# Moving three row loads and 28 operand loads in the queues of a streaming encoder's down projection

## The chip, the core and the metric

The kernel runs on one core of a Trainium2 chip. The metric is device time in microseconds (us) of one execution; three runs of the kernel before gave 2360.87, 2361.01 and 2362.78, a median of 2361.01. A core has a matmul engine (PE, with its weight loads as PEld), VectorE (DVE), ScalarE (ACT), GpSimd (POOL) and SyncE (SP). Each takes its instructions in the program's order and waits at an instruction until the semaphores that it names are reached. POOL and SP issue the transfers (DMA) of this kernel; transfers from POOL go through one queue of descriptors, those from SP through another.

## The reference, cut to what matters

One layer of a hybrid encoder: layer norm, a token mixer (a gated recurrence beside latent attention), a residual with layer norm, a convolutional feed-forward block, and again a residual with layer norm. 512 prompt frames and 32 running frames pass together, 544 columns. The part that the change touches is the end:

```python
u = x @ w_up                                   # (T, 2048) @ (2048, 5632)
a = conv_b + sum(ext[:, j:j + T] * conv_w[j] for j in range(3))
h = silu(a) * (x @ w_gate)
ff = h @ w_down                                # (T, 5632) @ (5632, 2048)
y = layer_norm(ALPHA * x + ff, ln2_g, ln2_b)
```

## The kernel before

Everything is held transposed: 128 rows of a feature by 544 columns. All numbers are 32-bit floats. A matmul in full 32-bit precision is made of three fast ones: each operand is split into a rounded high part and the low rest (`wh`, `wl` for weights), and high x high, high x low and low x high are added up in PSUM.

**Seven products.** The two large projections of the feed-forward block use a scheme of the Strassen kind. Weight and data are each cut in 2 x 2 blocks, and seven products of sums of blocks (`ORDER`: 11, s1, s2, s4, s3, 12, 22) take the place of eight. The sums on the data side are made once and stored in DRAM (`op_dr`, read back by `load_op`, line 1824, into the tiles `op11`, `ops1`, ... with two buffers each). The sums on the weight side are made in place, in the four blocks of the weight piece: class `Blocks`. For s1, DVE adds block 12 to block 11 (`plus`, line 1209), and then 22 is added to 12 by a transfer that accumulates (`plus_dma`, line 1212, issued by POOL, reading the weight from DRAM again); this sum is needed for product s3. For s2, DVE adds 22 to 11. When s2 has been split, a second accumulating transfer adds 21 to 11; this sum is needed for product 22. So each weight piece has two adding transfers. The rest of its loads are issued by SP in `pump` (line 1179) as soon as one of the eight slots `raw0` to `raw5`, `rawl0`, `rawl1` is free.

**The down projection.** Its depth of 5632 is cut in five chunks `g` of 1024 rows and a rest of 512 rows. Its 2048 output rows are cut in four groups `q` of 512 rows. A chunk takes the four groups one after the other, seven products each (in the last chunk, the products of the 512-row rest, line 118, are mixed in), so chunk 0 has the products 0 to 27, counted from `NU`, the first product of the down projection. A product is 24 matmuls (class `Twin`, line 1288) and then one DVE instruction that adds it to the group's output tile `y0` to `y3` (128 partitions x 4 x 544). These tiles hold the residual rows first: `load_y` reads them from DRAM (`x1_dr`, line 1830), and the first products of chunk 0 add on top of ALPHA times them (line 1864; later ones by line 1866). The tiles `y1` and `y2` use the two slots `eg` in which the up projection kept its gated rows, `y3` the slot `ea`. The last `eg` tiles are stored to DRAM by SP (`hd`, line 1542) before `y1` and `y2` can be loaded into their place.

**What sets the order.** PE, DVE and ACT follow an order written by hand in `play`. After product n, the weights of product n + 2 are split (ACT makes `wh`, line 1198; DVE makes `wl`, line 1199), the sums for product n + 3 are formed, then the hooks of n run, and `pump` issues loads. A hook is a function hung on a product with `at(n, f)`; it sets only where an instruction stands in the program. A load that a hook issues waits for its tile's slot and for nothing else of that product, so POOL runs through its list as far as the waits let it. POOL's list in the down projection holds adding transfers, operand loads of the next chunk and loads of output rows, in one order.

Of the kernel before, what the change touches and what calls it, by code (L numbers as in the profile page):

```python
# [59 lines left out]
def tile_encoder_step(ctx, tc, xp, xs, w_in, w_in4, w_kr, w_q_b, w_kv_b, w_out, w_up, w_gate, w_down, w_down2,  # L60
# [3 lines left out]
    V, A, G, PE = nc.vector, nc.scalar, nc.gpsimd, nc.tensor  # L64
    dma = nc.sync.dma_start
# [1074 lines left out]
    x1_dr = [dram.tile([P, HK, T], F32, name=f"x1d{b}", tag=f"x1d{b}") for b in range(2)]  # L1140
# [8 lines left out]
    def op_tile(name, i):  # L1149
        return home[name].tile([P, 2, 4, NI], R, name=f"op{name}{i}", tag=f"op{name}{i}")  # L1150
# [491 lines left out]
    with tc.manual_schedule():  # L1642
# [174 lines left out]
        ysq = [None] * 4  # L1817
# [4 lines left out]
        def load_op(g, name):  # L1822
            t = op_tile(name, g % 2)
            G.dma_start(t[:, :, :CHUNKS[g]].bitcast(F32), op_dr[g][:, STORED.index(name)])
            sets[g][name] = (t,)

        def load_y(q):
            ysq[q] = ff.tile([P, 4, T], F32, name=f"y{q}", tag=("ohl", "eg", "eg", "ea")[q],
                             bufs=2 if q in (1, 2) else 1)
            G.dma_start(ysq[q], x1_dr[q // 2][:, 4 * (q % 2):4 * (q % 2) + 4])  # L1830

        SPLIT = len(CHUNKS) - 1
        FIRST = ("11", "s1", "s2", "s3", "22")
# [66 lines left out]
        class Last:  # L1900
            g, name, time = None, "11", 3.0
# [26 lines left out]
        NU = len(items)  # L1928
        L4 = 4 * len(ORDER)
# [25 lines left out]
        def at(n, f):  # L1955
            hooks.setdefault(n, []).append(f)
# [41 lines left out]
        for i, name in enumerate(ORDER):  # L1998
            at(NU - 13 + 2 * i, lambda name=name: load_op(0, name))
        at(NU - 10, lambda: load_y(0))  # L2000
        for q in (1, 2, 3):
            at(NU + 4, lambda q=q: load_y(q))
        for g in range(1, len(CHUNKS)):
            for i, name in enumerate(ORDER):
                at(NU + (g - 1) * L4 + 3 * i + 1, lambda g=g, name=name: load_op(g, name))
        for (g, q), c in STAGED_AT.items():
            at(NU + L4 * g + 7 * q + 5, lambda c=c: stage_tail(c))
        at(n4 + 2, stage_hid)
# [383 lines left out]
```

## Time and profile before

| | |
|---|---|
| median of three runs | 2361.01 us |
| the profiled execution's own time | 2360.37 us |
| its span, first to last instruction | 2358.6 us |
| mean granted clock of the matmul engine | 0.993 |
| busy: PE | 2307.1 us, 98% |
| busy: DVE | 1702.0 us, 72% |
| busy: ACT | 1074.4 us, 46% |
| SP's queue: share of 16 DMA engines | 37.2% |
| POOL's queue: share of 16 DMA engines | 21.9% |

The span is what the trace covers; the execution's own time has 1.8 us around it. Most of the profile's groups are PE's matmuls of the up, gate and down projections (lines 1257 and 1288) and the splits of weights on ACT and DVE (lines 1198 and 1199). The down projection begins at 1843 us of the span. A row of waits says which engine and line waited for which; a row of stages says how long each engine was busy in a stretch of time; a row of the timeline shows in brackets how long the engine was idle ahead of an instruction and what ended that.

### The profile page before, as it was taken

How to read it: one execution, taken by the hardware profiler on the slowest of the kernel's cores; microseconds unless marked ns; L12 is line 12 of the kernel's file. 1: busy time of each engine (PE TensorE's matmuls, PEld its weight loads, DVE VectorE, ACT ScalarE, POOL GpSimd, SP SyncE). 2: the span in 40 equal slices, each digit the busy share in tenths (PEclk: the TensorE clock that was granted, in tenths of full speed). 3: DMA queues.
4: the chain of work that ended last, by engine and by line, in shares of the span. 5: the costliest groups of instructions: out<-in, count | busy, mean ns of one | idle time of the engine just before them, and what ended most of it. 6: DMA issues, size and time to landing. Idle time of an engine off the chain costs nothing.

```text
span 2358.6 us, 44463 instructions
## 1 busy us (share of the span) xinstructions
PE 2307.1 (98%) x18340; PEld 2290.6 (97%) x18340; DVE 1702.0 (72%) x2357; ACT 1074.4 (46%) x1652; POOL 222.1 (9%) x279
## 2 busy tenths in 40 slices
PE   7999999999999999999999999999999899999996
PEld 7999999999999999999999999999999899999996
DVE  7455578777786358987777777777776677777776
ACT  6345434343452237665555555555554333333323
POOL 1010000000001111010000100001001111111102
PEclk9999999999999999999999999999999999999998
DMA  7332263222245236787676776777768988889832
GB/s 244 100 101 77 72 205 104 93 81 80 80 159 186 90 114 221 197 216 225 172 204 202 181 228 170 205 201 182 228 169 249 354 260 298 276 272 310 271 94 78
DMA packets 155963, 427.47 MB, mean 181 GB/s; under 512 B 14192, under 2 KB 70256, under 8 KB 148464
## 3 DMA queue, kind: packets, MB, share of 16 engines
q1 hardware_dynamic: 129200, 299.97, 37.2%
q0 software_dynamic: 26560, 124.66, 21.9%
q8 instruction: 144, 2.36, 0.4%
q14 instruction: 59, 0.48, 0.1%
HBM read 351.75 MB, written 70.11 MB: 179 GB/s over the span
## 4 chain that ended last, share of the span: by engine, by line
PE 80%; issue 12%; DMA 3%; DVE 2%; ACT 2%; POOL 1%; ACTq 0%; POOLq 0%; SPq 0%; DVEq 0%
PE main L1257 22%; PE acc L1257 17%; PE main L118 13%; PE main L788 11%; PE acc L118 5%; PE main L1288 2%; PE s L853 2%; DMA raw<-in_w_down 2%; PE acc L1288 1%; PE main L555 1%; PE at L616 1%; PE at L585 1%; DMA x<-in_xp 1%; POOL raw L1212 1%; ACT wh L1198 0%
## 5 line engine op out<-in xcount | busy, mean ns | idle before, releaser
L1199 DVE TENSOR_TENSOR wl<-raw,wh 128x1024 fp32r<-128x1024 f32 x353 | 431.8, 1223 | 209.9 <-ACT wh L1198 209.7
L1198 ACT ACTIVATE wh<-raw 128x1024 fp32r<-128x1024 f32 x353 | 372.6, 1059 | 404.1 <-PE main L1257 99.2
L1257 PE MATMUL main<-op,wh 128*128 128x272 f32 x1408 | 265.4, 287 | 0.0
L1257 PE MATMUL acc<-ops,wh 128*128 128x272 f32 x1344 | 254.1, 287 | 0.0
L1257 PE MATMUL main<-ops,wh 128*128 128x272 f32 x1344 | 254.1, 287 | 0.0
L1257 PEld LDWEIGHTS main<-op,wh 128*128 128x128 f32 x1408 | 221.0, 188 | 0.0
L1257 PEld LDWEIGHTS acc<-ops,wh 128*128 128x128 f32 x1344 | 211.1, 188 | 0.0
L1257 PEld LDWEIGHTS main<-ops,wh 128*128 128x128 f32 x1344 | 211.0, 188 | 0.0
L1257 PE MATMUL main<-op,wl 128*128 128x272 f32 x704 | 202.9, 288 | 0.3 <-DVE wl L1199 0.3
L1257 PE MATMUL main<-ops,wl 128*128 128x272 f32 x672 | 193.7, 288 | 0.0
L1257 PE MATMUL acc<-ops,wl 128*128 128x272 f32 x672 | 193.7, 288 | 0.0
L118 PE MATMUL main<-aH,wh 128*128 128x272 f32 (+2 forms) x736 | 176.0, 295 | 0.2 <-ACT wh L280 0.2
L118 PE MATMUL main<-aH,wl 128*128 128x272 f32 (+2 forms) x736 | 172.2, 291 | 1.8 <-DVE wl L281 1.8
L118 PE MATMUL main<-aL,wh 128*128 128x272 f32 (+2 forms) x736 | 171.7, 290 | 1.0 <-DVE aL L269 1.0
L1257 PE MATMUL acc<-op,wh 128*128 128x272 f32 x832 | 157.5, 288 | 1.0 <-ACT ea L1511 1.0
L1198 ACT ACTIVATE wh<-rawl 128x1024 fp32r<-128x1024 f32 x93 | 98.9, 1063 | 118.2 <-PE acc L1257 43.8
L107 DVE TENSOR_TENSOR wl<-raw,wh 128x1024 fp32r<-128x1024 f32 (+2 forms) x72 | 79.1, 1101 | 89.3 <-ACT wh L106 85.3
L732 ACT ACTIVATE wh<-raw 128x1024 fp32r<-128x1024 f32 x84 | 88.7, 1056 | 111.3 <-DVE raw L727 105.0
L1288 PE MATMUL main<-ops,wh 128*128 128x272 f32 x656 | 127.4, 292 | 11.0 <-DVE y L1864 9.8
L1199 DVE TENSOR_TENSOR wl<-rawl,wh 128x1024 fp32r<-128x1024 f32 x93 | 113.8, 1223 | 27.0 <-ACT wh L1198 26.9
L1257 PEld LDWEIGHTS main<-op,wl 128*128 128x128 f32 x704 | 132.2, 188 | 0.5 <-DVE wl L1199 0.5
L1257 PEld LDWEIGHTS acc<-op,wh 128*128 128x128 f32 x832 | 130.4, 188 | 1.2 <-ACT ea L1511 1.2
(448 smaller groups left out, 6002.0 us busy)
## 6 DMA issues: line engine op xcount, KB each, us to landing
raw<-in_w_in SPq DMA_DIRECT2D x76, 512.0 KB, 3.6
raw<-in_w_up SPq DMA_DIRECT2D x71, 512.0 KB, 5.3
raw<-in_w_gate SPq DMA_DIRECT2D x71, 512.0 KB, 4.8
raw<-in_w_down SPq DMA_DIRECT2D x67, 512.0 KB, 8.7
opd<-ohl SPq DMA_DIRECT2D x20, 1088.0 KB, 5.5
ops<-opd POOLq DMA_DIRECT2D x20, 1088.0 KB, 12.3
raw<-in_w_out SPq DMA_DIRECT2D x40, 512.0 KB, 3.6
raw<-in_w_up POOLq DMA_DIRECT2D x35, 512.0 KB, 5.3
```

The lines of the kernel that those rows point to most:

```text
L107: V.tensor_tensor(out=dst(lv), in0=src(rv), in1=dst(hv).bitcast(F32), op=ALU.subtract)
L118: PE.matmul(ps, ww[:, wcols[0]:wcols[1]], aa[:, hs[j]], start=first and i == 0, stop=last and i == 2, skip_group_check=True)
L555: PE.matmul(ps[:, j * 512:j * 512 + 256], l[k][:, a:b], r4(w[:, k:k + 1, :])[:, 0, :, 128:256], start=k == 0 and i == 0, stop=k == 1 and i ...
L585: PE.matmul(sc[:, :nk], qn[j][:, q0:q0 + P], kn[j][:, :nk], start=True, stop=False)
L616: PE.matmul(po[:, :P], vt[:, k, j, :], t[:, k * P:(k + 1) * P], start=k == 0, stop=k == b)
L732: A.activation(wh, self.src, AF.Copy)
L788: PE.matmul(out, ww[:, k * P:(k + 1) * P], aa, start=name in ("11", "s1", "12") and k == 0 and q == 0, stop=k == HK - 1 and q == 2, skip_g ...
L853: PE.matmul(ps[:, j * 64:(j + 1) * 64], Kp[:, a:b], Qv[:, j * bt:(j + 1) * bt, 1, :], start=True, stop=True)
L1198: A.activation(wh, src, AF.Copy)
L1199: V.tensor_tensor(out=wl, in0=src, in1=wh.bitcast(F32), op=ALU.subtract)
L1257: PE.matmul(ps, ww[:, k * P:(k + 1) * P], aa, start=self.first and k == 0 and i == 0, stop=k == n - 1 and i == 2, skip_group_check=True)
L1288: PE.matmul(banks[:, 512 * u:512 * u + NI], ww[:, (u * n + k) * P:(u * n + k + 1) * P], aa, start=self.first and k == 0 and i == 0, stop=k ...
```

## The change

The loads of `y2` and `y3` are issued by SP instead of POOL, at hooks 8 and 10 instead of 4. `y1` stays on POOL at hook 4. The seven operand loads of the next chunk stand at hooks 1, 2, 8, 9, 15, 16 and 22 of a chunk instead of 1, 4, 7, 10, 13, 16 and 19. This holds for chunks 0 to 3, each loading for the chunk behind it, 28 loads in all. No work is added or left out.

```diff
         def load_y(q):
             ysq[q] = ff.tile([P, 4, T], F32, name=f"y{q}", tag=("ohl", "eg", "eg", "ea")[q],
                              bufs=2 if q in (1, 2) else 1)
-            G.dma_start(ysq[q], x1_dr[q // 2][:, 4 * (q % 2):4 * (q % 2) + 4])
+            (dma if q > 1 else G.dma_start)(ysq[q], x1_dr[q // 2][:, 4 * (q % 2):4 * (q % 2) + 4])
...
         at(NU - 10, lambda: load_y(0))
-        for q in (1, 2, 3):
-            at(NU + 4, lambda q=q: load_y(q))
+        for q, n in ((1, 4), (2, 8), (3, 10)):
+            at(NU + n, lambda q=q: load_y(q))
         for g in range(1, len(CHUNKS)):
             for i, name in enumerate(ORDER):
-                at(NU + (g - 1) * L4 + 3 * i + 1, lambda g=g, name=name: load_op(g, name))
+                at(NU + (g - 1) * L4 + 7 * (i // 2) + 1 + i % 2, lambda g=g, name=name: load_op(g, name))
```

The first place is POOL's list at the start of chunk 0. `raw3` and `raw2` on line 1212 are the two adding transfers of group q=1 (12 += 22, then 11 += 21), lines 1824 are operand loads for chunk 1, lines 1830 the loads of output rows:

```order
 L1212 DMA raw4_20226<-in_w_down 128x1024
 L1824 DMA op111_20589<-opd1_8255 128x2176
-L1830 DMA y1_20691<-x1d0_8252 128x2176
-L1830 DMA y2_20693<-x1d1_8253 128x2176
-L1830 DMA y3_20695<-x1d1_8253 128x2176
-L1824 DMA ops11_20697<-opd1_8255 128x2176
+L1824 DMA ops11_20624<-opd1_8255 128x2176
+L1830 DMA y1_20693<-x1d0_8252 128x2176
 L1212 DMA raw3_20387<-in_w_down 128x1024
 L1212 DMA raw2_20355<-in_w_down 128x1024
```

Ahead of the adding transfers of q=1 stood three loads of output rows and two operand loads; now there are two operand loads and one load of output rows.

The second place is SP's list at the same time. Lines 1179 are weight loads (`raw3` and `raw1` here are blocks 11 and 12 of group q=3), line 1542 the last store of gated rows, from the `eg` slot that `y2` takes:

```order
 L1542 DMA hd_8267<-eg_20323 128x2x544
-L1179 DMA raw4_20689<-in_w_down 128x1024
-L1179 DMA rawl1_20823<-in_w_down 128x1024
-L1179 DMA raw3_20854<-in_w_down 128x1024
+L1179 DMA raw4_20691<-in_w_down 128x1024
+L1179 DMA rawl1_20817<-in_w_down 128x1024
+L1830 DMA y2_20819<-x1d1_8253 128x2176
+L1179 DMA raw3_20852<-in_w_down 128x1024
 L1179 DMA raw1_20885<-in_w_down 128x1024
+L1830 DMA y3_20887<-x1d1_8253 128x2176
 L1179 DMA raw2_20918<-in_w_down 128x1024
```

The loads of `y2` and `y3` now stand among SP's weight loads, three places and six places behind the store. The weight loads keep their order (only their numbers differ).

The third place is POOL's list in chunk 1, around the two adds of group q=2 (`raw2`, then `rawl1`), with the operand loads for chunk 2:

```order
-L1824 DMA ops20_21685<-opd2_8256 128x2176
-L1824 DMA ops40_21781<-opd2_8256 128x2176
-L1212 DMA raw2_21558<-in_w_down 128x1024
-L1824 DMA ops30_21881<-opd2_8256 128x2176
+L1824 DMA ops20_21717<-opd2_8256 128x2176
+L1824 DMA ops40_21750<-opd2_8256 128x2176
+L1212 DMA raw2_21560<-in_w_down 128x1024
 L1212 DMA rawl1_21527<-in_w_down 128x1024
+L1824 DMA ops30_21944<-opd2_8256 128x2176
 L1824 DMA op120_21977<-opd2_8256 128x2176
```

The operand load that stood between the two adds now stands behind the second, so that operand loads come in pairs behind a group's adds.

## The prediction

> **What bounds the kernel now.** First the waits of the matmul engine in the down projection (from 1838 us to the end; columns: who waited for whom, total us, times, longest):
>
> ```profile
> PE main L1288 <- DVE y L1864: 9.8, 1, 9.8
> PE main L2203 <- ACT rt L2086: 2.5, 1, 2.5
> ...
> PE main L1288 <- DVE y L1866: 1.2, 1, 1.2
> ```
>
> PE is busy elsewhere; only the first and the last row shown lie in the products of the down projection (L1288). The rest is the closing normalisation, which the change does not touch. So nearly all that can be won here is one stall of 9.8 us. Next the stages around it (length, then busy us and count of PE, PEld, DVE, ACT, POOL, then granted clock, DMA share, GB/s):
>
> ```profile
> 1856.00:1862.00 6.00, 6.00 (x50) 6.00 (x49) 5.02 (x6) 1.95 (x3) 0.00 (x0) 1.00 1.01 410
> 1862.00:1868.00 6.00, 6.00 (x50) 6.00 (x49) 4.81 (x6) 2.76 (x3) 1.60 (x4) 1.00 0.62 221
> 1868.00:1874.00 6.00, 6.00 (x50) 6.00 (x49) 2.41 (x3) 0.34 (x1) 2.34 (x3) 1.00 0.96 386
> 1874.00:1880.00 6.00, 2.33 (x19) 2.12 (x17) 0.00 (x0) 0.00 (x0) 0.55 (x1) 1.00 1.03 303
> 1880.00:1886.00 6.00, 0.00 (x0) 0.00 (x0) 1.84 (x3) 2.46 (x3) 0.00 (x0) 0.61 1.04 312
> 1886.00:1892.00 6.00, 5.83 (x27) 5.87 (x28) 3.04 (x5) 0.84 (x2) 0.00 (x0) 0.53 1.01 415
> 1892.00:1898.00 6.00, 6.00 (x50) 6.00 (x50) 5.72 (x6) 2.83 (x3) 1.41 (x2) 1.00 0.17 29
> ```
>
> PE stops in the fourth row, and when it comes back it runs at half clock: 27 matmuls in 5.83 us instead of 50 in 6. The transfers are dense during the stall, but thin just ahead of it (0.62). The chain of waits says for what PE waited (start, length, what):
>
> ```profile
> 1855.30 2.90 PE main L1288 x23
> ...
> 1867.98 14.99 DMA raw<-in_w_down
> 1883.08 1.06 ACT wh L1198
> ...
> 1885.31 0.72 DVE y L1864
> 1886.17 5.57 PE main L1288 x23
> ```
>
> It waited for an adding transfer (12 += 22 of row group q=1, L1212) that took 15 us to land. POOL's own timeline shows why (start, length, line, count, idle ahead and what ended it):
>
> ```profile
> 1847.61 0.89 POOL L1212 DMA_DIRECT2D raw<-in_w_down  x1 [4.42 <-DVE wl L1199]
> 1848.16 0.88 POOL L1824 DMA_DIRECT2D op<-opd  x1
> 1848.74 0.84 POOL L1830 DMA_DIRECT2D y<-x1d  x1
> 1866.26 1.06 POOL L1830 DMA_DIRECT2D y<-x1d  x2 [16.68 <-DVE y L1864]
> 1867.31 0.53 POOL L1824 DMA_DIRECT2D ops<-opd  x1
> 1867.98 1.80 POOL L1212 DMA_DIRECT2D raw<-in_w_down  x2
> ```
>
> POOL stood 16.68 us at the load of y2. The releaser named, a DVE addition, writes another tile; it merely ended last. y2 takes the slot of the last `eg` tile, which is free when its store to `hd` (SP, issued 1855.83) has landed, 9.8 us later by the row below, at 1865.6. So both adding transfers of q=1 waited twice: at issue behind y2's wait, and in POOL's ring behind y2, y3 and an operand, 1,088 KB each.
>
> **The change part by part.** *What the stall costs.* It has two terms. The idle time itself is 9.84 us:
>
> ```profile
> 1886.17 0.79 PE L1288 MATMUL main<-ops,wh 128*128 128x272 f32 x2 [9.84 <-DVE y L1864]
> ```
>
> The slow clock is the second: 23 matmuls took 5.57 us after it and 2.90 us before it (chain), so 2.67 us. Together 12.51 us, the most that this place can give. The clock was still 1.00 up to 1880, 3.7 us after PE stopped at 1886.17 - 9.84 = 1876.33; a remaining stall shorter than that should cost its own length alone. The Trainium skill, "TensorE: Matmul & The Clock Gate", Part 1, says the clock halves after an idle window of about 3.4 us and returns after as long at work; its estimate for the second term would be 1.7 us and the forecast 1.0 us higher. The measured 2.67 stands in the sum.
>
> *y2 and y3 leave POOL.* The adding transfer can now be issued when VectorE has read its block:
>
> ```profile
> 1860.57 1.23 DVE L1209 TENSOR_TENSOR raw<-raw,raw 128x1024 f32<-128x1024 f32 x1
> ```
>
> This ends at 1861.80, so the issue is at about 1861.9 instead of 1867.98: 6.1 us sooner. Ahead of it in POOL's ring stand an operand (1848.16), the second operand (`s1`, new ahead of y1) and y1. Three landing rows price the way (us from issue to landing, least/median/greatest: of the y1 load issued at 1848.74, of the two adds issued at 1867.98 and 1868.62, and of the `hd` store):
>
> ```profile
> DMA to landing us min/median/max: 15.0/15.0/15.0
> DMA to landing us min/median/max: 15.0/15.9/16.8
> DMA to landing us min/median/max: 9.8/9.8/9.8
> ```
>
> y1 landed at 1863.7. SP's last load issued in that stretch (1858.09, landing in 8.7 us, below) landed at 1866.8. The two adds landed at 1883.0 and 1885.4, so one add holds the ring some 2.5 us. An operand of 1,088 KB (1.11 MB) at the 410 GB/s of the first stage is 2.7 us.
>
> ```profile
> 1855.83 0.64 SPq L1542 DMA_DIRECT2D hd<-eg  x1
> 1858.09 0.33 SPq L1179 DMA_DIRECT2D raw<-in_w_down  x1
> 1869.72 0.33 SPq L1179 DMA_DIRECT2D rawl<-in_w_down  x1
> DMA to landing us min/median/max: 8.7/8.7/8.7
> ```
>
> Since the engines were full until about 1866.8, the new operand ends at 1866.8 + 2.7 and the add at 1866.8 + 2.7 + 2.5 = 1872.0. It was needed 3.20 us (1886.17 - 1882.97) ahead of PE's 1876.33, at 1873.1. So it lands 1.1 us in time and the term is 0. Bounds: at best POOL's ring goes on from y1 alone, 1863.7 + 5.2 = 1868.9, also 0. At worst both take twice as long because SP's ring shares the engines: 1866.8 + 10.4 = 1877.2, a stall of 4.1 us. I take 0, since SP has nothing left in its ring at 1866.8 and sends only one 512 KB load (1869.72) and y2 behind it.
>
> *What comes next.* The second add of q=1 (2.5 us behind, 1874.5) is needed two products later; a product, 24 matmuls, takes 3.0 us (24/23 of the 2.90 in the chain), so at 1876.33 + 6.0 - 3.2 = 1879.1. The add of q=2 is issued 3.6 us into product 12, as now in product 5 (1858.2 to 1861.8), at 1882.9. From 1872.0 the engines have to move the second add (2.5), two operands and y2 and y3 (4 x 2.7), three 512 KB loads (1.3 each at 410 GB/s), then this add (2.5): 19.7 us, 1891.7. It is needed at 1876.33 + 7 x 3.0 - 3.2 = 1894.1. The term is 0 again; at the 303 to 312 GB/s of the stall's rows all takes a third longer, 1898.2, a stall of 4.1 us.
>
> *y2 and y3 on SP.* y2 is issued behind the load of 1869.72, at about 1870.1 (its store has landed by then). With the 5.4 to 15.0 us that y loads took it lands between 1875.5 and 1885.1; the first addition into it is due at the end of product 14, 1888.4, and PE notices only at product 16, 1891.4. Behind it on SP wait the blocks 11 and 12 of q=3 (`raw3`, `raw1`), not due before product 19, about 1900; their slots come free earlier too, because the adds do. y3 is due at 1909.4. Cost 0; every us that y2 lands after 1891.4 would cost PE a us.
>
> *The operand loads in pairs.* In later groups one load now stands between the two adds of a group; afterwards none does. What this does is seen in two places of chunk 1, since both patterns are there already. ACT's rows:
>
> ```profile
> 1990.92 1.06 ACT L1198 ACTIVATE wh<-raw 128x1024 fp32r<-128x1024 f32 x1 [1.90 <-PE main L1288]
> 1996.69 1.06 ACT L1198 ACTIVATE wh<-rawl 128x1024 fp32r<-128x1024 f32 x1 [4.71 <-DMA rawl<-in_w_down]
> ```
>
> and POOL's:
>
> ```profile
> 1965.56 1.41 POOL L1824 DMA_DIRECT2D ops<-opd  x2
> 1979.92 0.90 POOL L1212 DMA_DIRECT2D raw<-in_w_down  x1 [12.95 <-DVE rawl L1209]
> 1980.47 0.90 POOL L1824 DMA_DIRECT2D ops<-opd  x1
> 1986.50 0.86 POOL L1212 DMA_DIRECT2D rawl<-in_w_down  x1 [5.13 <-DVE wl L1199]
> ```
>
> Behind a pair (1965.56) the next add comes 14 us later and ACT waits for PE, as it should; with a load between the adds (1980.47) ACT waits 4.71 us for the second add. PE did not stop there, so moving the load wins 0 now; it only widens a margin. Bounds: a gain of 1.2 us (the last row of the waits), a loss of as much.
>
> *Sum.* 2360.37 us for the profiled execution (span 2358.6) less 12.51 is 2347.86. The median of the runs shown, 2361.01, lies 0.64 above that execution: 2348.5 us.
>
> **The rivals.** *B, a short stall remains.* Both worst cases, 4.1 and 4.1 us, hardly add up, since a stall at the first place delays the need at the second. For it speaks that the first margin is 1.1 us only. 1.5 to 6 us: 2350 to 2354.5.
>
> *C, the transfers themselves are the bound.* The engines were full (1.01 to 1.04) through the stall, and no byte is taken away. Then only the gap of 1862 to 1868 can be used, 6 x (1 - 0.62) = 2.3 us, the slow clock stays, and the time is 2358.7. Against it: PE waits for 512 KB and not for all that moves, and the 0.17 of 1892 to 1898 shows that the backlog ends. The Trainium skill, "DMA: Bandwidth & Descriptors", "Issuing engines are not separate DMA queues", has a rule on this side: all issuers share the same 16 engines, and a second issuer saves only the time to issue. By it the two loads would save POOL's 1.06 us. Traffic rows agree with the sharing; POOL's 16.68 us is what the rule leaves out.
>
> *D, slower.* With both operand loads right behind a group's adds, POOL's ring could be longer when the next group's first add is issued. It decides from the point where that add lands over 3 us later than now, in each of the 16 groups: 1 us each makes 2364.5. Against it stands the pair at 1965.56, gone when the next add came.
>
> That the change doesn't do what it says is excluded by the order of instructions shown.
>
> **How the numbers follow.** No stall over 1.5 us: 0.65 (2347 to 2350); B 0.19; C 0.10; D 0.06. A difference of 0.2% (4.7 us) is what a measurement here can tell, so A and B are faster (0.84), C the same (0.10), D slower (0.06). The range goes from 2346.5, with 1.2 us more gained and 0.8 for the scatter, to 2354.5, the end of B; outside are C and D.
>
> **What would show it.** Right: no PE wait near 8 us on L1288, the clock at 1.00 after 1876, POOL issuing the first add of q=1 near 1862 and it landing before 1873, no idle of 16.68 us on POOL. Wrong: the add issued early and still landing after 1876 (C), DVE waiting for y2, or several waits of PE near 1 us behind pairs of operand loads (D).

## The result and the profile after

The changed kernel takes 2346.88 us, the median of four runs (2345.76 to 2347.67); the kernel before takes 2360.94 (four runs, 2360.62 to 2362.78). The medians differ by 14.1 us, where the prediction had 12.5 us less. The ratio, estimated from all the runs, is 0.9938 with a 95% interval of 0.9921 to 0.9956; by it the gain is 14.6 us and the time 2346.3, just under the forecast's range of 2346.5 to 2354.5, while the median lies just inside. The profiled execution of the changed kernel took 2347.67 us, its span 2345.9.

The waits of PE in the down projection and after it (from 1838 us; who waited for whom, total us, times, longest), to be read beside the first rows of the prediction:

```profile
PE main L2203 <- ACT rt L2086: 2.5, 1, 2.5
...
```

No row names L1288 any more. Both waits of the products are gone: the one of 9.8 us, which the prediction was about, and the one of 1.2 us (product 123), which it left standing. What is left belongs to the closing normalisation. The stages around product 11 (length; busy us and count of PE, PEld, DVE, ACT, POOL; granted clock, DMA share, GB/s):

```profile
1864.00:1870.00 6.00, 6.00 (x50) 6.00 (x50) 4.81 (x6) 2.77 (x3) 0.87 (x1) 1.00 1.02 376
1870.00:1876.00 6.00, 6.00 (x50) 6.00 (x50) 3.55 (x5) 2.17 (x3) 2.00 (x3) 1.00 1.01 227
1876.00:1882.00 6.00, 6.00 (x51) 6.00 (x50) 4.43 (x6) 2.11 (x3) 0.00 (x0) 1.00 1.01 427
1882.00:1888.00 6.00, 6.00 (x51) 6.00 (x50) 5.68 (x7) 2.26 (x3) 0.87 (x1) 1.00 1.02 420
1888.00:1894.00 6.00, 6.00 (x51) 6.00 (x49) 5.24 (x6) 2.12 (x2) 1.98 (x3) 1.00 1.03 299
```

PE works without a gap and the clock stays at 1.00. The DMA engines have no thin stretch here: every row is at 1.01 to 1.03, where the kernel before had 0.62 ahead of its stall and 0.17 behind it. POOL's timeline shows the cause (start, length, line, count, idle ahead and what ended it):

```profile
1864.14 0.87 POOL L1212 DMA_DIRECT2D raw<-in_w_down  x1 [11.65 <-DVE raw L1209]
1870.27 0.89 POOL L1212 DMA_DIRECT2D raw<-in_w_down  x1 [5.25 <-DVE wl L1199]
1870.82 1.44 POOL L1824 DMA_DIRECT2D ops<-opd  x2
1885.20 0.87 POOL L1212 DMA_DIRECT2D rawl<-in_w_down  x1 [12.93 <-DVE raw L1209]
1891.78 0.87 POOL L1212 DMA_DIRECT2D raw<-in_w_down  x1 [5.71 <-DVE wl L1199]
```

POOL now waits for the DVE addition on which the adding transfer depends, and no longer for the slot of y2. The two loads of output rows are in SP's timeline:

```profile
1857.76 0.42 SPq L1542 DMA_DIRECT2D hd<-eg  x1
...
1872.59 0.86 SPq L1830 DMA_DIRECT2D y<-x1d  x1
...
1878.20 0.43 SPq L1830 DMA_DIRECT2D y<-x1d  x1
```

The changed kernel's rows of the times from issue to landing are, in this order, those of the first and the second add of q=1, of the `hd` store, of y2, and of the first and the second add of q=2:

```profile
DMA to landing us min/median/max: 9.5/9.5/9.5
DMA to landing us min/median/max: 6.1/6.1/6.1
DMA to landing us min/median/max: 14.8/14.8/14.8
DMA to landing us min/median/max: 13.0/13.0/13.0
DMA to landing us min/median/max: 9.6/9.6/9.6
DMA to landing us min/median/max: 9.4/9.4/9.4
```

**Where the time came from.** The products of the down projection (L1288, with the start of the first matmul and of the last) in the profile before and in the one after:

```profile
L1288 PE MATMUL main<-op,wh x656: 283/288/369, 1843.1 to 2307.4; 128*128 128x272 f32 x164
L1288 PE MATMUL main<-op,wh x656: 283/288/369, 1845.0 to 2295.1; 128*128 128x272 f32 x164
```

From 1843.1 to 2307.4 are 464.3 us, from 1845.0 to 2295.1 are 450.1: 14.2 us less between the same two matmuls, which agrees with the difference of the medians (14.1). Of these the stall was 9.84, the slow clock behind it 2.67, the wait at product 123 1.2; 0.5 stays unassigned. The spans of the two profiled executions differ by 12.7 only, mainly because the down projection began 1.9 us later in the second of them. The cause lies far ahead of anything the change touches; the last section shows it.

### The profile page after: what moved, and what is told of

Its sections match the earlier page's. It is cut to its first block, busy times and chain, and to the rows that moved or that the text cites. A ratio compares the mean times of both kernels' runs of the same rounds, so it can differ in the third digit from the quotient of the medians.

```text
span 2345.9 us, 44466 instructions
## 1 busy us (share of the span) xinstructions
PE 2305.4 (98%) x18340; PEld 2289.3 (98%) x18340; DVE 1703.1 (73%) x2357; ACT 1075.3 (46%) x1652; POOL 221.4 (9%) x277
## 4 chain that ended last, share of the span: by engine, by line
PE 95%; DVE 1%; ACT 1%; DMA 1%; issue 1%; POOL 0%; ACTq 0%; SPq 0%; DVEq 0%
PE main L1257 22%; PE acc L1257 17%; PE main L118 13%; PE main L788 11%; PE main L1288 11%; PE acc L1288 7%; PE acc L118 5%; PE s L853 2%; PE main L555 1%; PE at L616 1%; PE at L585 1%; DMA x<-in_xp 1%; PE main L542 0%; PE at L587 0%; DMA raw<-in_w_in 0%
## 5 line engine op out<-in xcount | busy, mean ns | idle before, releaser
L1257 PE MATMUL main<-ops,wh 128*128 128x272 f32 x1344 | 254.1, 287 | 0.0
L1257 PEld LDWEIGHTS main<-ops,wl 128*128 128x128 f32 x672 | 126.3, 188 | 0.0
```

The source lines that it names most:

```text
L1257: PE.matmul(ps, ww[:, k * P:(k + 1) * P], aa, start=self.first and k == 0 and i == 0, stop=k == n - 1 and i == 2, skip_group_check=True)
```

## The experiments

All times are medians, and each comparison is with the kernel before on the same chip: 2361.22 us for the first four kernels (19 runs), 2361.00 for the last three (13 runs). Experiments 1, 2 and 7 start from the kernel before, 3 to 6 from the changed kernel. Waits, starts and landing times are those of the profiled execution.

**1. The output rows alone.** The operand loads stay as before.

```diff
-            G.dma_start(ysq[q], ...)
+            (dma if q > 1 else G.dma_start)(ysq[q], ...)
-        for q in (1, 2, 3):
-            at(NU + 4, lambda q=q: load_y(q))
+        for q, n in ((1, 4), (2, 8), (3, 10)):
+            at(NU + n, lambda q=q: load_y(q))
```

> Only the output rows move (y2 and y3 to SP, hooks 8 and 10); operand loads stay at hooks 1, 4, 7, 10, 13, 16, 19. Theory: the stall of 9.8 us at product 11 and its slow clock (together 12.5 us) come from y2 and y3 ahead of the adds on POOL, so this part alone brings them: 2348.4 us, no PE wait near 9.8 us; the short wait of 1.2 us at product 123 stays, because a single operand load still stands between the two adds of a group. Rival (the pairs of operand loads make the gain): the stall stays and the time is above 2358. Rival (the transfers are the bound): a stall of about 7.5 us stays, 2358.7.

2350.01 us (2349.36 to 2351.18), ratio 0.9955 (0.9940 to 0.9970): 11.2 us less by the medians, and 1.6 us above the expected 2348.4. The long stall is gone, but PE waits at two places, of which one was expected. Its row of the waits (total, times, longest):

```profile
PE main L1288 <- DVE y L1866: 2.8, 2, 1.5
```

and its timeline at both places, with the wait in brackets:

```profile
1904.95 0.49 PE L1288 MATMUL main<-op,wh 128*128 128x272 f32 x2 [1.53 <-DVE y L1866]
2216.12 0.37 PE L1288 MATMUL main<-ops,wh 128*128 128x272 f32 x1 [1.30 <-DVE y L1866]
```

The second is product 123, where the kernel before waited too. The first, at product 20, is new. ACT's timeline says what it waited for:

```profile
1901.86 2.01 ACT L1198 ACTIVATE wh<-raw 128x1024 fp32r<-128x1024 f32 x2 [6.47 <-DMA raw<-in_w_down]
```

and POOL's timeline when that transfer was issued:

```profile
1883.87 0.86 POOL L1824 DMA_DIRECT2D ops<-opd  x1
1889.89 0.88 POOL L1212 DMA_DIRECT2D raw<-in_w_down  x1 [5.17 <-DVE wl L1199]
```

The row of its time to landing:

```profile
DMA to landing us min/median/max: 11.9/11.9/11.9
```

It is the second add of q=2. With an operand load (1883.87) between it and the first add it took 11.9 us to land; with that load moved behind it (the changed kernel) it takes 9.4. So the paired operand loads are worth 2350.01 - 2346.88 = 3.1 us once the long stall is gone (2.9 when each kernel is compared with its own runs of the kernel before), and the two waits add up to 2.8.

**2. The pairs alone.** The three loads of output rows stay on POOL at hook 4.

```diff
-                at(NU + (g - 1) * L4 + 3 * i + 1, ...)
+                at(NU + (g - 1) * L4 + 7 * (i // 2) + 1 + i % 2, ...)
```

> Only the operand loads move to pairs behind the adds; y1, y2 and y3 stay on POOL at hook 4. Theory: POOL still stands at y2 until the store of the last gated rows has landed, and the adds of q=1 still follow y2 and y3, so the stall at product 11 stays at 9 to 11 us with its slow clock; only the 1.2 us wait at product 123 goes: 2359 to 2361 us. Rival (the pairs make the gain): 2347 to 2350.

2358.23 us (2354.51 to 2360.30, ten runs), ratio 0.9985 (0.9976 to 0.9994). PE's wait in the products:

```profile
PE main L1288 <- DVE y L1864: 8.8, 1, 8.8
```

POOL's timeline ahead of it:

```profile
1868.63 1.07 POOL L1830 DMA_DIRECT2D y<-x1d  x2 [17.81 <-DVE y L1864]
1869.87 1.80 POOL L1212 DMA_DIRECT2D raw<-in_w_down  x2 [0.17 <-issue]
```

The time lies a little below the 2359 to 2361 that were expected, the wait a little below the 9 to 11 us. The stall stays, 1.0 us shorter, which fits that the operand that stood between y3 and the adds is now ahead of y1: the first add takes 11.9 us to land instead of 15.0. The wait at product 123 is gone. With the first experiment this separates the two parts: the rows remove the stall and only the rows do; the pairs remove the wait at product 123 and only the pairs do.

How they remove it is not as the expectations have it. Product 123 lies in the last chunk, where no operand load is issued. In the kernel before, the last operand load between two adds is issued at 2170.03, in the last group of chunk 3; the second add behind it takes 10.0 us to land, and ACT waits for it:

```profile
2186.16 2.01 ACT L1198 ACTIVATE wh<-raw 128x1024 fp32r<-128x1024 f32 x2 [4.62 <-DMA raw<-in_w_down]
```

In the changed kernel the same add takes 7.4 us and ACT does not wait. The first add of the next group comes 22.4 us after the first add of this one with the load between (2169.47 to 2191.92), 21.0 without (2158.63 to 2179.65). One group later still, the add that product 123 needs takes 11.4 us to land instead of 9.8. That the one lateness makes the other is read from the order of events; no run tests it alone.

**3. y3 alone back on POOL at hook 4.** Now no load ahead of the adds has to wait for the `hd` store, but one more of 1,088 KB stands there.

```diff
-            (dma if q > 1 else G.dma_start)(ysq[q], ...)
+            (dma if q == 2 else G.dma_start)(ysq[q], ...)
-        for q, n in ((1, 4), (2, 8), (3, 10)):
+        for q, n in ((1, 4), (2, 8), (3, 4)):
```

> The changed kernel, but y3 goes back to POOL at hook 4, ahead of the adds; y2 stays on SP. y3's slot is free early, so POOL has no long wait and only its ring is longer, by one transfer of 1,088 KB. Theory (position in the ring, each transfer its own time): the first add of q=1 lands 2.7 to 3.5 us later than in the changed kernel, where 1.3 us were to spare, so PE waits 1.4 to 2.2 us, too short for the clock to fall: 2348.3 to 2349.5. Rival (only POOL's wait at y2 matters, not the ring): no wait, 2346.9. Rival (the bytes in flight are the bound): no wait either, since the same bytes move.

2348.27 us (2346.57 to 2350.46), ratio 0.9950 (0.9934 to 0.9967). PE's only wait in the products:

```profile
PE main L1288 <- DVE y L1864: 1.0, 1, 1.0
```

and the first add of q=1 in POOL's timeline:

```profile
1862.25 0.90 POOL L1212 DMA_DIRECT2D raw<-in_w_down  x1 [9.86 <-DVE raw L1209]
```

The add is issued as early as in the changed kernel but takes 11.9 us to land instead of 9.5, and PE waits 0.96 us at product 11. One row load ahead in the same queue costs 2.4 us of landing; 1.3 us of slack in the changed kernel swallow part of it. The expected wait, 1.4 to 2.2 us, was somewhat too long.

**4. y2 alone back on POOL at hook 4.** The one that waits for the `hd` store.

```diff
-            (dma if q > 1 else G.dma_start)(ysq[q], ...)
+            (dma if q == 3 else G.dma_start)(ysq[q], ...)
-        for q, n in ((1, 4), (2, 8), (3, 10)):
+        for q, n in ((1, 4), (2, 4), (3, 10)):
```

> The changed kernel, but y2 goes back to POOL at hook 4, ahead of the adds; y3 stays on SP. Theory: POOL stands at y2 until the store has landed (14 us after its issue in the changed kernel), then y2 goes ahead of the first add, which lands about 6 us later than it is needed: a PE wait of 5 to 7 us, after which the clock is at half for some microseconds: 2352.5 to 2357. Against the run with y3 ahead, the difference is the wait at issue. Rival (only the length of the ring matters): the same as with y3 ahead, 2348.3 to 2349.5.

2355.29 us (2353.21 to 2356.86, ten runs), ratio 0.9976 (0.9966 to 0.9985). PE's wait in the products:

```profile
PE main L1288 <- DVE y L1864: 5.6, 1, 5.6
```

and POOL's timeline at y2 and the adds:

```profile
1869.67 0.54 POOL L1830 DMA_DIRECT2D y<-x1d  x1 [18.11 <-DVE y L1864]
1870.40 1.80 POOL L1212 DMA_DIRECT2D raw<-in_w_down  x2 [0.19 <-issue]
```

POOL stands for 18.11 us at y2, both adds are issued together behind it, and most of the stall is back. Experiments 2, 3 and 4 take the stall apart by the lateness of the first add: with both rows ahead it comes 8.8 us too late, without y3 5.6, without y2 0.96, without both 1.3 us in time. So y2 weighs 8.8 - 0.96 = 7.8, y3 8.8 - 5.6 = 3.2, together 11.0 against 10.1 measured for both. Nearly all of y2's weight is the wait at issue: the first add takes 9.3 us to land here and 9.5 in the changed kernel, but it is issued 7.3 us later, counted from the last add of q=0 (21.9 us behind it, 14.6 in the changed kernel). The wait at issue is most of the stall; the queue behind it is the rest.

**5. Both rows late, but on POOL.** The positions are those of the change, the issuer is not.

```diff
-            (dma if q > 1 else G.dma_start)(ysq[q], ...)
+            G.dma_start(ysq[q], ...)
```

> The changed kernel, but y2 and y3 stay on POOL at hooks 8 and 10, behind the adds of q=1. Theory: the adds of q=1 are in time as in the changed kernel, no stall at product 11; y2, y3 and two operands (4 x 2.7 us) now all stand in POOL's ring ahead of the first add of q=2, which had 1.1 us to spare, so a wait of 0 to 2 us at product 18, without a fall of the clock: 2347 to 2349. Rival (the second queue makes the gain): a stall of over 5 us, above 2352.

2349.45 us (2348.94 to 2349.86), ratio 0.9950 (0.9935 to 0.9965). PE's longest wait in the products:

```profile
PE main L1288 <- DVE y L1864: 2.6, 1, 2.6
```

POOL's timeline up to the first add of q=2:

```profile
1870.94 0.56 POOL L1830 DMA_DIRECT2D y<-x1d  x1 [1.77 <-DMA hd<-eg]
1871.50 1.13 POOL L1824 DMA_DIRECT2D ops<-opd  x2
1872.63 0.53 POOL L1830 DMA_DIRECT2D y<-x1d  x1
1883.18 0.87 POOL L1212 DMA_DIRECT2D rawl<-in_w_down  x1 [10.03 <-DVE raw L1209]
```

and that add's time to landing:

```profile
DMA to landing us min/median/max: 13.6/13.6/13.6
```

Product 11 no longer waits, product 18 does, a little over the expected 0 to 2 us: the first add of q=2 now has two operands and two rows ahead of it in one queue and takes 13.6 us to land, 9.6 in the changed kernel. The bytes and the 16 engines are the same in both kernels; the queue in which y2 and y3 stand is worth 2.6 us.

**6. Both rows on SP, but at hook 4.** The issuer is that of the change, the positions are not.

```diff
-        for q, n in ((1, 4), (2, 8), (3, 10)):
-            at(NU + n, lambda q=q: load_y(q))
+        for q in (1, 2, 3):
+            at(NU + 4, lambda q=q: load_y(q))
```

> The changed kernel, but y2 and y3 are issued on SP at hook 4 instead of 8 and 10, right behind the last weight load that follows the store. Theory (what counts is that they are not ahead of the adds on POOL): no PE wait in the down projection, the time of the changed kernel, 2346.2 to 2347.8; SP stands at y2 until the store has landed and one weight load stands behind it, which is not due for 20 us. Rival (the later hooks are needed too): SP's weight loads come late, a PE wait of over 2 us, above 2349.

2347.19 us (2346.03 to 2349.84), ratio 0.9944 (0.9927 to 0.9960), which the four runs do not tell from the changed kernel. The group of SP's row loads (count, least/median/greatest duration in ns, first and last start):

```profile
L1830 SPq DMA_DIRECT2D y<-x1d x2: 327/1132/1936, 1870.9 to 1871.2; - x2
L1830 SPq EVENT_SEMAPHORE  x1: 10833/10833/10833, 1860.0 to 1860.0; - x1
```

SP stands 10.8 us at y2 (second row, 10833 ns) as POOL did before, and PE has no wait in the products. On SP the long wait is harmless, since what stands behind it is not due for that long. The later hooks are not what the change needs on SP.

**7. Output rows between the two adds.** The kernel before with y2 and y3 one hook later, still on POOL: the first add is free, the second stands behind them.

```diff
-        for q in (1, 2, 3):
-            at(NU + 4, lambda q=q: load_y(q))
+        for q, n in ((1, 4), (2, 5), (3, 5)):
+            at(NU + n, lambda q=q: load_y(q))
```

> The kernel before with one number changed: y2 and y3 at hook 5 instead of 4, still on POOL, so they stand between the first and the second add of q=1; operand loads as before. Theory: the first add is in time and the stall of 9.8 us at product 11 goes; the second add now has POOL's wait at y2 and two transfers ahead of it and lands 2.5 to 4 us later than product 13 needs; the waits that single operand loads cause (1.3 to 2.8 us in all) stay: 2350 to 2354. Rival (the wait only moves from the one add to the other with its size): a stall of about 10 us with its slow clock, 2358 to 2361.

2358.64 us (2355.11 to 2361.07, ten runs), ratio 0.9988 (0.9979 to 0.9998). This was a miss of the theory, which gave 2350 to 2354; the time is that of the rival, a wait that only moves (2358 to 2361). PE's longest wait in the products:

```profile
PE main L1288 <- ACT tw L1969: 7.7, 1, 7.7
```

POOL's timeline around the two adds of q=1:

```profile
1862.15 0.88 POOL L1212 DMA_DIRECT2D raw<-in_w_down  x1 [11.27 <-DVE raw L1209]
1871.19 1.07 POOL L1830 DMA_DIRECT2D y<-x1d  x2 [8.16 <-DMA hd<-eg]
1872.31 0.88 POOL L1212 DMA_DIRECT2D raw<-in_w_down  x1
```

and the second add's time to landing:

```profile
DMA to landing us min/median/max: 14.3/14.3/14.3
```

The first add is issued at 1862.15, as wanted, and product 11 does not wait. The second add is issued at 1872.31, when y2's wait is over, and takes 14.3 us behind the two rows; PE waits 7.7 us at product 13 instead, 1.0 us at product 123, and runs at half clock for a while (last section). The theory had priced the rows at 2.7 us each in the queue; they landed 6.9 and 11.0 us after their issue, 4.7 us apart, and the add 3.9 behind the second, while SP's weight loads shared the engines. Right was that y2's wait holds up whatever stands behind it; wrong was the price of the queue.

## Where the prediction was right, and which step was mis-sized

**The stall, right.** The step from POOL's 16.68 us of idle time to a late adding transfer was what happened, and its two numbers can be checked with the 1.9 us by which the profiled down projection began later. The first add was to be issued at 1861.9 (1863.8 after the shift; it was 1864.14) and to land at 1872.0 (1873.9; it was 1864.14 + 9.5 = 1873.6). A margin of 1.1 us was worked out, 1.3 measured. The term of 12.51 us for stall and slow clock came in full. That the landing came out to 0.3 us was partly luck. The prediction had the engines full until 1866.8 and SP's queue empty from then on. In the kernel before their share was 1.06 from 1863 to 1864 but 0.62, 0.23 and 0.05 in the three microseconds behind it; and in the changed kernel SP's store and its last weight load ran beside the add, landing at 1872.5 and 1873.8. The first error made the forecast of the landing later, the second sooner.

**The loads on SP, right.** y2 landed at 1872.59 + 13.0 = 1885.6, due at 1888.4 + 1.9. The store ahead of it took 14.8 us instead of 9.8, while the engines were full where they had been at 0.62; the margin covered that.

**The next place, q=2: half right.** The first add's margin was put at 2.4 us, it was 1.1. The second add of q=2 was not priced at all. In the changed kernel it has 0.8 us of slack, and with the rows alone (experiment 1) it is late by 1.5. By the trace the kernel before had 1.0 us there, but behind a stall of 9.84 us in which the queues caught up. Taking the stall away makes PE arrive at the next deadlines that much earlier, and every one of them has to be worked out again, not only the first.

**The operand loads in pairs, mis-sized.** This is the term that failed: "moving the load wins 0 now", with a bound of 1.2 us of gain. It measured 3.1 us, so that the sum came out some 1.6 us too long and the range ended too close on the fast side. Of the 3.1, 1.3 is the wait at product 123: it stood in the prediction as the upper bound and was then set to nothing, because the step looked at a place in chunk 1 where PE did not stop. Another 1.5 is the wait at product 20, which the rows alone bring out and the pairs keep away; 0.3 stays unassigned. The two errors partly cancel: the rows alone were worth 11.2 us and not 12.5, since that wait came with them, the pairs 3.1 and not 0; together about 14.1 and not 12.5.

**The rivals.** B (a short stall remains) did not occur in the changed kernel, though its relatives have one: 1.5 us at product 20 in experiment 1, 2.6 at product 18 in experiment 5, 0.96 at product 11 in experiment 3, without a fall of the clock in any of them. The prediction's limit of 3.7 us for that is not shown, though: in experiment 7 the clock fell 2.0 us after PE had stopped (last section). C (the transfers are the bound) falls: the engines are as full after as before, at 1.01 to 1.03, and PE does not wait; what counts is which of the transfers comes first. The Trainium skill, "DMA: Bandwidth & Descriptors", "Issuing engines are not separate DMA queues", says that a second issuer saves only the time of issuing. The runs agree that the queues share the engines (SP's store took 14.8 us instead of 9.8 with more of POOL's transfers beside it), but not with the "only": y2's wait and place on POOL cost 8.8 - 0.96 = 7.8 us, and the queue alone 2.6 us (experiment 5). D (pairs make the queue longer) falls: no wait of PE lies behind a pair.

## What to carry to other kernels

A load that must wait for its slot holds up everything that its engine issues behind it: look not at how late that load itself may be, but at what stands behind it and when that is due. When a stall is taken away, work out the slack of each later deadline again at the new pace, since a stall also pays for the lateness behind it; a margin read where the engine did not stop does not stand for the places that the stall had covered. Among transfers that share full engines, put the one with the nearest deadline ahead of those that only fill a buffer.

## What the runs showed of the chip that was not expected

**Short waits cost little beyond their length, long ones more.** PE's waits of 0.96, 1.3, 1.5 and 2.6 us were followed by no fall of the granted clock. Those of 5.6 (experiment 4), 7.7 (experiment 7), 8.8 (experiment 2) and 9.84 us were followed by half clock for 6.8, 10.2, 6.8 and 10.2 us. Experiment 4's windows show one of them (columns as above):

```profile
1880.00:1883.00 3.00, 0.11 (x1) 0.14 (x1) 2.11 (x3) 2.51 (x3) 0.00 (x0) 0.50 1.04 326
1883.00:1886.00 3.00, 3.00 (x14) 3.00 (x15) 2.64 (x3) 0.34 (x1) 0.00 (x0) 0.50 1.01 425
1886.00:1889.00 3.00, 3.00 (x24) 3.00 (x24) 0.94 (x2) 1.31 (x2) 0.00 (x0) 0.91 1.01 417
```

PE is back at work just before 1883, yet the clock is at 0.50 through the next row and part of the one behind it: 14 matmuls in 3 us instead of 25. Both lengths are multiples of 3.4 us, and the fall came 2.0 to 5.0 us after PE had stopped, so the extra cost of a long stall is not a fixed sum. Product 11 took 4.7 us here from its first matmul to that of product 12, 5.5 in the kernel before and 4.5 in experiment 2, instead of 3.0: 1.7, 2.5 and 1.5 us. (The 2.67 of the prediction is the 2.5 and 0.16 that this count puts to the stall; their sum is the same.) The Trainium skill, "TensorE: Matmul & The Clock Gate", Part 1, describes windows of about 3.4 us that run freely; the lengths agree with it, and the 1.7 us that the prediction estimated from it fits this stall but not the one before.

How long a wait is safe is not shown: no run has one between 2.6 and 5.6 us, and the soonest fall is that of experiment 7, where PE stopped at 1882.15:

```profile
1883.00:1886.00 3.00, 0.00 (x0) 0.00 (x0) 0.00 (x0) 0.00 (x0) 0.00 (x0) 0.70 1.04 364
```

With half clock to the end of the row, its mean of 0.70 puts the fall at 1884.2, 2.0 us after the stop. The wait of 2.6 us in experiment 5 passed without a fall, so the length of a wait alone does not decide.

**Half clock far ahead of the change moves whole executions.** One stretch near the start, of the kernel before:

```profile
31.00:38.00 7.00, 7.00 (x60) 7.00 (x60) 6.93 (x14) 2.46 (x6) 0.86 (x2) 0.98 0.16 45
```

and of the changed one:

```profile
31.00:38.00 7.00, 7.00 (x52) 7.00 (x52) 6.93 (x14) 1.51 (x4) 0.86 (x2) 0.82 0.06 14
```

The change touches nothing there, but the clock was 0.82 in the second against 0.98 (0.69 against 0.78 in the 7 us ahead of it, and 0.72 against 1.00 between 732 and 738 us), and the down projection began at 1845.0 instead of 1843.1. The same matmuls start 0.04 us later in the second at 30 us, 0.97 at 35, 0.99 at 730 and 1.9 from 738 on, so that these two places make the whole difference. Of the nine profiled executions, the three with half clock near 733 us (the changed kernel, experiments 4 and 6) begin the down projection at 1844.0 to 1845.0, the other six at 1842.9 to 1843.2. Differences below 2 us between two profiled executions of this kernel are therefore read from the stretch in question, not from the span.

**The same bytes take different times to land.** The same store took 9.8 us in the kernel before and 14.8 in the changed one, and the first add of q=2 took 9.6 or 13.6 us with the same bytes in all, by the queue that two loads stood in.
